# Two attention stages of a diffusion block: stages one step apart, SBUF divided by phase, TensorE in the emitted order

## The chip, the core and the metric

The kernel is one program on one core of a Trainium2 chip. The core has a matrix engine (PE, TensorE; PEld are its weight loads), a vector engine (DVE), a scalar engine (ACT), a general engine (POOL, GpSimd) and a queue engine (SP) from which most DMAs are issued. They run side by side, each through its own list of instructions in order, and wait for one another by semaphores. The metric is the device time of one execution in microseconds; lower is better.

## The reference

Two layers over 512 latent tokens and 256 context tokens of width 1024, all in float32. Layer 0 mixes tokens by differential attention (8 heads, each with two query and key maps of 64 and values of 128), layer 1 by a neighbourhood attention (16 heads, here in 8 groups of two). Each is followed by an MLP with hidden width 4096.

```python
def diff_attend(q, k, v, lam):                                  # layer 0
    s = einsum('bqhmd,bkhmd->bhmqk', q, k) * ATTN_SCALE          # two maps m
    p = softmax(s)
    return einsum('bhqk,bkhe->bqhe', p[:, :, 0] - lam * p[:, :, 1], v)
# layer 1, each query row: a window of keys with a bias and a mask, and all context keys
prob = softmax(concat([where(col_in, s_loc + bias, -inf), s_ctx]))
o = p_loc @ v_band + p_ctx @ v_c
# both layers
q, k = rms_norm(q, q_gain), rms_norm(k, k_gain)                  # per head, over 64
x = x + mod[2] * (o @ w_o)
x = x + mod[5] * (square(relu(modulate(rms_norm(x), mod[3], mod[4]) @ w1)) @ w2)
# mod = silu(c) @ w_mod + b_mod: six sections of 1024 columns for each layer
```

## The kernel before

Tokens lie in six tiles of 128 (two of context, four latent). A float32 product is done in three passes of a high and a low part, so every weight tile has a copy W[:, 0] (ACT, L99) and a remainder W[:, 1] (POOL, L100); its raw form arrives in a tile R, of which there are two. The loops are unrolled.

- **Start** (0 to 66 us): the first norm, the first modulation chunks and head 0's projections (`first_head`).
- **Layer 0 attention** (to 444 us): for each of 8 heads `qkv0` projects six token tiles (L346, 24 products of 384 columns each), norms q and k (`qk_normed`, L350), rotates them on POOL (L412 to L416), transposes (`turn`, L424) and splits them (`q_split`, `k_split`). `attend0` works on six query tiles: scores into the only PSUM tile S (L458), maxima (L463), exponentials (L464), the difference of the two maps (L470), transposes (L478), their split (L480, L481), the product with the values (L485), and the norm of the output (L487 to L494), which goes to DRAM as oT (L501).
- **Output projection, residual and norm** (`project`, L651), partly beside head 7's attention; then **MLP 0** (561 to 1111 us, L719 up and L753 down) with 24 modulation chunks beside it (L200 to L213), each one's weights loaded by SP.
- **Layer 1 attention** (1180 to 1495 us): `qkv1` and `attend1` for 8 groups, four units each (L575 to L618), with the bias by DMA (L514) and its mask added on POOL (L517). Then its projection, and **MLP 1** to the end.

What sets the order: the streams are Python generators, and `run` steps them by a string of letters (`ORD_HEAD` for a head, `ORD_GROUP` for a group), so that the projections of head h+1 are emitted among the attention of head h. This order gives only priorities. A planner (`schedule_with_timeline_sim=True`) simulates the engines and puts each engine's instructions, PE's too, in the order in which it finds them ready. A tile tag has a fixed number of buffers: five W of 1024 columns for the whole program, four N, seven Y, two each of E and X. One head's weights are four W. A new tile waits for the release of an old one.

Of the kernel before, what the change touches and what calls it, by code (L numbers as in the profile page):

```python
# [10 lines left out]
F32 = mybir.dt.float32  # L11
# [7 lines left out]
P = 128  # L19
D = 1024  # L20
# [14 lines left out]
# the order of the interleaved streams, by letters (see run)  # L35
ORD_FIRST = "aa"
# [13 lines left out]
class Block:  # L50
    def __init__(self, tc, ctx, a):
# [6 lines left out]
        self.wpool = pool("wpool", 5)  # L58
# [5 lines left out]
    BUFS = {"H": 8, "Q": 8, "E": 2, "X": 2, "N": 4, "Y": 7, "O": 4, "T": 2, "SQ": 12, "SA": 12, "SO": 8, "V": 1, "C4": 1}  # L64

    def sbt(self, tag, shape, dt=F32):
        self.n += 1
        return self.sb.tile(shape, dt, tag=tag, name=f"{tag}{self.n}", bufs=self.BUFS[tag])

# [21 lines left out]
    def wload(self, src, n, tile=None, eng=None):  # L91
        """a weight slice [128, n] as its float32r parts: [:, 0] high, [:, 1] low."""
# [4 lines left out]
        if w is None:  # L97
            w = self.wpool.tile([P, 2, 1024], F32R, tag="W", name=self._name("W"))
# [4 lines left out]
    def mod_load(self, l, n, early=False):  # L103
        """256 columns of the modulation matrix, as eight k-tiles."""
        src = self.a["wmod"][l, n]
        if early:
            w = self.wpool.tile([P, 2048], F32, tag="W", name=self._name("W"))
# [9 lines left out]
    def setup(self):  # L117
# [13 lines left out]
        # silu(c), silu(c_ctx), padded to 32 columns  # L131
# [8 lines left out]
        # modulation scalars: [layer][norm] -> A (gain*(1+scale)), B (shift)  # L140
# [28 lines left out]
        # lambda  # L169
# [221 lines left out]
    def qkv0(self, w, hT, out, accs=None, tag='Q'):  # L391
# [37 lines left out]
        for i, t in ((0, None), (1, None), (2, 0), (3, None), (4, 2), (5, None)):  # L429
            tile_(i)  # L430
            yield
            if t is not None:
                turn(t)
                yield
# [520 lines left out]
```

## Time and profile before

| | |
|---|---|
| runs | 1925.61, 1935.61, 1938.24 us; median 1935.61 |
| span of the profiled execution | 1928.0 us, 7.6 below the median; no other time is given for that execution |
| PE busy | 1809.4 us (94%) over 10256 matmuls |
| DVE, ACT, POOL busy | 1205.3, 812.5, 770.6 us (63%, 42%, 40%) |
| mean granted PE clock | 0.977 |
| HBM | 95 GB/s over the span |

A group row of the profile has line, engine, operation, output and inputs, shape and count; then the busy time, the mean in ns of one, and the engine's idle time before them with who ended it. A row of a windows view has the stretch, its length, the busy time and instruction count of PE, PEld, DVE, ACT and POOL, the granted PE clock, DMA share and GB/s. A row of a timeline has start and length in us. Matmuls overlap in the pipeline, so the time that one costs is the distance between starts, which is shorter than its listed duration. The heads' periods are read from the seven stores of oT (L501), the groups' from those of L621, of which those used here are at 223.8, 275.6, 327.5, 379.8 and 429.9 us, and at 1253.2, 1289.8, 1334.0, 1374.9, 1416.1 and 1458.0 us.

### The profile page before, as it was taken

The numbers are of one execution on the slowest core, as the hardware profiler recorded it, in microseconds if no ns is written. First come the engines' busy times: TensorE is split into PE (matmuls) and PEld (weight loads), VectorE is DVE, ScalarE is ACT, GpSimd is POOL, SyncE is SP. The second block draws the span as 40 slices with busy tenths as digits, with TensorE's granted clock in tenths as the row PEclk, the third lists the DMA queues.
The fourth block names the chain that finished last, engine by engine and source line by source line (L and its number), as shares of the span: only waits on it lengthen the run. The fifth ranks groups of instructions, "written<-read, shape, count | busy, mean of one in ns | idle before, by whom it ended". The sixth has DMA issues, their size and how long they took to land.

```text
span 1928.0 us, 27111 instructions
## 1 busy us (share of the span) xinstructions
PE 1809.4 (94%) x10256; PEld 1574.1 (82%) x10256; DVE 1205.3 (63%) x2349; ACT 812.5 (42%) x1819; POOL 770.6 (40%) x620
## 2 busy tenths in 40 slices
PE   6899999997899999999999988998998989999998
PEld 5788888885688888888888968998897778888886
DVE  4688888887664343343334685988889664444447
ACT  4466666666342221221221244666656342232231
POOL 3655555544222221221222443444543334344443
PEclk9999999998999999999999998999998999999999
DMA  7222222225222332332432241223323223323331
GB/s 296 92 67 71 86 85 74 73 69 195 84 89 90 118 120 91 128 124 95 131 113 74 57 125 41 50 62 74 77 72 99 93 77 100 97 87 94 103 94 71
DMA packets 58723, 185.02 MB, mean 96 GB/s; under 512 B 7328, under 2 KB 13792, under 8 KB 54496
## 3 DMA queue, kind: packets, MB, share of 16 engines
q1 hardware_dynamic: 52848, 173.44, 29.1%
q10 hardware_dynamic: 5744, 9.85, 1.4%
q8 instruction: 80, 1.31, 0.3%
q14 instruction: 51, 0.42, 0.1%
HBM read 174.45 MB, written 8.81 MB: 95 GB/s over the span
## 4 chain that ended last, share of the span: by engine, by line
PE 67%; DVE 15%; DMA 6%; ACT 4%; POOL 4%; issue 4%; SPq 1%; ACTq 0%; POOLq 0%; DVEq 0%
PE PD L719 23%; PE PA L753 11%; PE PB L753 10%; PE PA L346 9%; PE PA L651 4%; PE PA L200 2%; DMA X<-in_rpb_dram 2%; PE PS L458 2%; PE PB L485 1%; POOL W L100 1%; PE PQ L335 1%; DVE SA L581 1%; DMA N<-oT 1%; DMA R<-in_wmod_dram 1%; DVE N L604 1%
## 5 line engine op out<-in xcount | busy, mean ns | idle before, releaser
L100 POOL TENSOR_TENSOR W<-R,W 128x1024 fp32r<-128x1024 f32 (+1 forms) x200 | 451.0, 2262 | 700.8 <-ACT W L99 700.7
L99 ACT ACTIVATE W<-R 128x1024 fp32r<-128x1024 f32 (+1 forms) x204 | 200.9, 994 | 457.8 <-PE PB L753 364.2
L719 PE MATMUL PD<-Q,W 128*128 128x384 f32 (+1 forms) x1584 | 291.4, 332 | 1.1 <-DVE Q L270 0.5
L719 PEld LDWEIGHTS PD<-Q,W 128*128 128x128 f32 x1584 | 269.5, 188 | 16.6 <-issue 7.0
L346 PE MATMUL PA<-W,H 128*128 128x384 f32 x1008 | 201.8, 347 | 5.1 <-DVE T L209 4.4
L728 DVE TENSOR_TENSOR N<-N 128x768 f32<-128x768 f32 (+1 forms) x64 | 61.9, 969 | 220.3 <-ACT N L727 110.7
L346 PE MATMUL PA<-W,Q 128*128 128x384 f32 (+1 forms) x1008 | 186.7, 332 | 10.9 <-DVE H L535 5.6
L719 PE MATMUL PD<-H,W 128*128 128x512 f32 (+1 forms) x816 | 187.6, 386 | 3.4 <-DVE H L271 2.5
L346 PEld LDWEIGHTS PA<-W,H 128*128 128x128 f32 x1008 | 176.3, 191 | 13.0 <-DVE T L209 4.9
L719 PEld LDWEIGHTS PD<-H,W 128*128 128x128 f32 x816 | 148.9, 191 | 36.3 <-DVE H L271 2.7
L346 PEld LDWEIGHTS PA<-W,Q 128*128 128x128 f32 x1008 | 162.7, 198 | 13.3 <-DVE H L535 7.0
L753 PE MATMUL PA<-W,H 128*128 128x512 f32 x648 | 168.1, 399 | 2.7 <-DVE T L759 2.5
L233 POOL TENSOR_TENSOR SQ<-SQ,half 128x4 f32<-128x4 f32 (+1 forms) x96 | 93.9, 979 | 161.0 <-DVE SQ L231 133.9
L753 PEld LDWEIGHTS PA<-W,H 128*128 128x128 f32 x648 | 119.2, 188 | 32.9 <-issue 6.2
L753 PE MATMUL PB<-W,H 128*128 128x512 f32 x504 | 132.3, 394 | 0.0
L753 PE MATMUL PA<-W,Q 128*128 128x512 f32 x432 | 108.7, 391 | 2.2 <-ACT Q L730 1.7
L753 PEld LDWEIGHTS PB<-W,H 128*128 128x128 f32 x504 | 94.5, 188 | 19.4
L764 DVE TENSOR_TENSOR H<-PA,H 128x512 f32<-128x512 f32 x78 | 53.7, 688 | 78.6 <-PE PA L753 78.6
L753 PEld LDWEIGHTS PA<-W,Q 128*128 128x128 f32 x432 | 80.9, 188 | 21.1 <-ACT Q L730 2.4
L464 ACT ACTIVATE E<-PS,SA 128x768 f32<-128x768 f32 (+1 forms) x96 | 72.7, 758 | 34.4 <-DVE SA L463 33.8
L463 DVE TENSOR_REDUCE SA<-PS 128x1 f32<-128x768 f32 (+1 forms) x96 | 74.4, 775 | 20.2 <-ACT E L464 13.6
L753 PE MATMUL PB<-W,Q 128*128 128x512 f32 x336 | 85.3, 389 | 0.0
(213 smaller groups left out, 3177.1 us busy)
## 6 DMA issues: line engine op xcount, KB each, us to landing
R<-in_w_dram SPq DMA_DIRECT2D x128, 512.0 KB
W<-in_wmod_dram SPq DMA_DIRECT2D x32, 1024.0 KB
R<-in_wmod_dram SPq DMA_DIRECT2D x32, 512.0 KB
R<-in_wqa_dram SPq DMA_DIRECT2D x32, 384.0 KB
R<-in_wqb_dram SPq DMA_DIRECT2D x32, 384.0 KB
X<-in_rpb_dram SPq DMA_DIRECT2D x48, 128.0 KB
R<-in_woa_dram SPq DMA_DIRECT2D x8, 512.0 KB
R<-in_wob_dram SPq DMA_DIRECT2D x8, 512.0 KB
```

Of the source, the lines that this page charges most:

```text
L99: nc.scalar.activation(w[:, 0, :n], raw, AF.Copy)
L100: (eng or nc.gpsimd).tensor_sub(w[:, 1, :n], raw, w[:, 0, :n].bitcast(F32))
L200: nc.tensor.matmul(ps[32 * q:32 * q + 32, 0:256], self.silu[:, kt, :], raws[kt], start=kt < 4, stop=kt >= 4)
L233: nc.gpsimd.tensor_tensor(r, ss, self.half[:, :n], op=ALU.pow)
L346: nc.tensor.matmul(acc[:, :n], hT[kt][:, x, P * i:P * i + P], w[kt // 2][:, y, o:o + n], start=(kt == 0 and p == 0), stop=(kt == KT - 1 an ...
L463: nc.vector.tensor_reduce(mx, s, op=ALU.max, axis=AX, negate=True)
L464: nc.scalar.activation(e[:, m, :nk], s, AF.Exp, bias=mx[:, 0:1], accum_out=sm[:, m:m + 1])
L651: nc.tensor.matmul(ps, oHL[h][:, x, c:c + P], w[h // 2][:, y, 512 * (h % 2):512 * (h % 2) + 512], start=(h == hs[0] and p == 0), stop=(h = ...
L719: nc.tensor.matmul(ps[:, at:at + b1 - b0], w[kt // 4][:, x, o:o + P], hT[kt][:, y, b0:b1], start=(kt == 0 and p == 0), stop=(kt == KT - 1 ...
L728: nc.vector.tensor_mul(r, r, r)
L753: nc.tensor.matmul(ps, hd[:, x, P * i - c0:P * i - c0 + P], w[f][:, y, 512 * n:512 * n + 512], start=(f == 0 and p == 0), stop=(f == len(h ...
L764: nc.vector.tensor_add(av, ps, av)
```

## The change

It keeps the arithmetic and regroups it. (1) `sbuf_phase` gives W, N and a new tag OT to pools that are opened and closed with four phases: five W of 1024 columns and four N at the start and around both MLPs, eight W of 768 and two OT in layer 0's attention, six W of 768 and four N in layer 1's. Y has six buffers in place of seven. (2) `attend0` and `attend1` are cut into the stages scores (0), turned (1) and weigh (2), emitted in the order of ATT0 and ATT1; `qkv0` and `qkv1` step in halves of a token tile; the last turn of a head is emitted inside the next head's loop (`p`), and the first two tiles of a group inside the group before (`r`). A head's weights are asked for one loop earlier. (3) Both loops run under `manual_schedule` for PE: its instructions keep the emitted order; the other engines' are still placed by the planner. The start, the first group's projections, both output projections and both MLPs are outside it. (4) Some DVE operations change: the addition of EPS after the q and k norm's sum becomes a 65th column of that sum, four operations become `scalar_tensor_tensor`, and the copy at L385 moves to POOL. (5) Four of the 24 modulation chunks beside MLP 0 move to the end of layer 1's attention. The output projection steps in four and three heads.

```diff
-ORD_HEAD = "qlalmqmaqqaqbqqbqaAQ"
-ORD_OUT0 = "lmlmaqaqaqAQ"
-ORD_GROUP = "qaqqaqaqaqAQ"
-ORD_OUT1 = "aqaqaqaAQ"
+ORD_HEAD = "aa qq aa q p q l a q a q m l a qq a q aaa q m aaa qq a q b a q aa"
+ORD_OUT0 = "q l aaaa p a m l a m a q a q aaa q aaa qq a q a qq aa Q"
+ORD_FIRST1 = "qqqqqqqqqqqq rr q a"
+ORD_GROUP = "qq a q a qq a a q a q a aa qqq a a r q a r b"
+ORD_GROUP7 = "qq a q a qq a a q a q a aa l qqq a a m q a b"
+ORD_OUT1 = "q a l a m a l aa m a q aa q a q a qq a l m Q"
+MODS_LATE = 4
+ATT0 = ((0, 1), (1, 0), (2, 0), (1, 1), (2, 1), (0, 2), (0, 3), (1, 2), (2, 2), (0, 4), (1, 3), (2, 3),
+        (0, 5), (1, 4), (2, 4), (1, 5), (2, 5))
+ATT1 = ((0, 1), (1, 0), (2, 0), (0, 2), (1, 1), (2, 1), (0, 3), (1, 2), (2, 2), (1, 3), (2, 3))
...
+    def sbuf_phase(self, name, wcols, **tags):
+        with ExitStack() as st:
+            self.wcols, self.bufs = wcols, tags
+            self.room = {tag: st.enter_context(self.tc.tile_pool(name=name + tag, bufs=n, reuse_waits="tile"))
+                         for tag, n in tags.items()}
+            yield
...
     def qk_normed(self, acc, ns):
-        sq = self.sbt('Y', [P, n])
-        nc.scalar.activation(sq, raw, AF.Square, scale=0.125)
+        nc.scalar.activation(self.sq[:, :ns, 0:64], xn, AF.Square, scale=0.125)
-        nc.vector.tensor_reduce(ss, sq.rearrange("p (a b) -> p a b", b=64), op=ALU.add, axis=AX)
-        r = self.rstd(ss, ns, 'SQ')
-        nc.vector.tensor_mul(xn, xn, r[:, :, None].to_broadcast([P, ns, 64]))
+        nc.vector.tensor_reduce(ss, self.sq[:, :ns], op=ALU.add, axis=AX)
+        r = self.power(ss, ns, 'SQ')
+        nc.vector.scalar_tensor_tensor(xn, xn, 1.0, r[:, :, None].to_broadcast([P, ns, 64]),
+                                       op0=ALU.mult, op1=ALU.mult)
...
-            nc.vector.tensor_copy(kl[b, m, cols], kl[a, m, cols].bitcast(F32))
+            nc.gpsimd.tensor_copy(kl[b, m, cols], kl[a, m, cols].bitcast(F32))
...
+        for i in range(NT):
+            acc = self.pst('A')
+            for half in range(2):
+                self.qkv_matmul(acc, half, w, hT, i, 0, 384)
+                if half == 1:
+                    tile_(i, acc)
+                yield
+                if (i, half) in ((3, 0), (4, 1)):
+                    turn(0 if i == 3 else 2)
+                    yield
         turn(4)
         yield
...
-            nc.vector.tensor_scalar_mul(on, o, ro[:, 0:1])
+            nc.vector.scalar_tensor_tensor(on, o, ro[:, 0:1], self.one[:, 0:1].to_broadcast([P, P]),
+                                           op0=ALU.mult, op1=ALU.mult)
...
+        scores(0)
+        yield
+        for stage, i in ATT0:
+            (scores, turned, weigh)[stage](i)
             yield
         turn(*late.pop(0))
...
-                nc.vector.tensor_sub(u[:, 1, :], r, u[:, 0, :].bitcast(F32))
+                nc.vector.scalar_tensor_tensor(u[:, 1, :], r, 1.0, u[:, 0, :].bitcast(F32),
+                                               op0=ALU.mult, op1=ALU.subtract)
...
-            for h in range(1, HEADS0):
-                nxt = []
-                qkv = b.qkv0(w if h == 1 else b.load_qkv(a["wqa"], h), hT, nxt)
-                att2 = b.attend0(h, nxt, last if h + 1 == HEADS0 else None)
-                run(mods, ORD_HEAD, q=qkv, a=att, b=att2)
-                att = att2
+            run(mods, "a", a=att)
+            ahead = iter(())
+            with tc.manual_schedule(engines={mybir.EngineType.PE}):
+                for h in range(1, HEADS0):
+                    nxt = []
+                    qkv = b.qkv0(w, hT, nxt)
+                    if h + 1 < HEADS0:
+                        w = b.load_qkv(a["wqa"], h + 1)
+                    att2 = b.attend0(h, nxt, last if h + 1 == HEADS0 else None)
+                    run(mods, ORD_HEAD, q=qkv, a=att, b=att2, p=ahead)
+                    att, ahead = att2, qkv
...
+                if len(mods.todo) > MODS_LATE:
+                    mods.load(True)
+                    mods.chunk()
...
+            with tc.manual_schedule(engines={mybir.EngineType.PE}):
+                for g in range(1, GROUPS1):
+                    att2 = b.attend1(g, nxt, last if g + 1 == GROUPS1 else None)
+                    qkv, nqkv, nxt = nqkv, None, []
+                    if g + 1 < GROUPS1:
+                        nqkv = b.qkv1(b.load_qkv(a["wqb"], g + 1), hT1, nxt)
+                    run(mods, ORD_GROUP if nqkv else ORD_GROUP7, q=qkv, r=nqkv, a=att, b=att2)
+                    att = att2
```

The fourth operation that becomes `scalar_tensor_tensor` is the copy of 64 columns at L589.

More of the change, by code (lines that the diff above doesn't have):

```diff
@@ L619, in attend1 @@
+        scores(0)
+        yield
+        for stage, u in ATT1:
+            (scores, turned, weigh)[stage](u)
+            if (stage, u) != ATT1[-1]:
                 yield
@@ L671, in project @@
             ps = self.pst('A')
[L672 removed]
+            part(ps, w0, i, range(4), final=False)
+            yield
+            part(ps, w0, i, range(4, KT - 1), first=False)
             gated(ps, x, i, 0, x)
```

245 lines of the change are left out of this document (137 added, 108 removed).

## The prediction

> **What bounds the kernel now.** I read the page first, then the windows view over whole periods, then PE's timeline for the price of one matmul, and last DVE's groups and the chain of waits.
>
> ```profile
> PE 1809.4 (94%) x10256; PEld 1574.1 (82%) x10256; DVE 1205.3 (63%) x2349; ACT 812.5 (42%) x1819; POOL 770.6 (40%) x620
> ...
> PE 67%; DVE 15%; DMA 6%; ACT 4%; POOL 4%; issue 4%; SPq 1%; ACTq 0%; POOLq 0%; DVEq 0%
> ```
>
> PE is busy for 94%, which leaves 119 us, yet a third of the chain that ended last is not PE's. The two don't fit, because a listed matmul is longer than what it costs. So I price PE's work by distances between starts. The windows view gives the sums over five chunks of MLP 0 (698.35 to 883.2), four heads (223.8 to 429.9) and five groups (1253.2 to 1458.0), and one group:
>
> ```profile
> sum 184.85, PE 184.85 PEld 158.09 DVE 70.51 ACT 39.13 POOL 47.71; mean PE 36.97 PEld 31.62 DVE 14.10 ACT 7.83 POOL 9.54
> ...
> sum 206.10, PE 193.52 PEld 175.49 DVE 170.85 ACT 136.91 POOL 109.24; mean PE 48.38 PEld 43.87 DVE 42.71 ACT 34.23 POOL 27.31
> ...
> sum 204.80, PE 189.54 PEld 184.46 DVE 177.57 ACT 129.67 POOL 94.65; mean PE 37.91 PEld 36.89 DVE 35.51 ACT 25.93 POOL 18.93
> ...
> 1289.80:1334.00 44.20, 39.20 (x264) 38.45 (x263) 36.22 (x88) 26.63 (x68) 19.46 (x20) 0.92 0.24 60
> ```
>
> PE's timeline, in MLP 0, a head and a group:
>
> ```profile
> 738.89 0.50 PE L213 MATMUL PA<-sel,T 128*128 128x2 f32 x4
> 739.25 8.05 PE L719 MATMUL PD<-Q,W 128*128 128x384 f32 x45
> 747.24 1.07 PE L200 MATMUL PA<-W,silu 128*32 128x256 f32 x16
> 748.24 1.65 PE L753 MATMUL PA<-W,H 128*128 128x512 f32 x6
> 749.73 2.96 PE L753 MATMUL PB<-W,H 128*128 128x512 f32 x12
> 752.52 0.88 PE L719 MATMUL PD<-Q,W 128*128 128x384 f32 x4
> ...
> 257.99 0.49 PE L478 MATMUL PB<-ident,E 128*128 128x128 f32 x3
> 258.23 1.30 PE L346 MATMUL PA<-W,H 128*128 128x384 f32 x6
> ...
> 263.24 1.59 PE L485 MATMUL PB<-Q,X 128*128 128x256 f32 x12
> 264.67 0.27 PE L446 MATMUL PB<-ident,O 128*128 128x128 f32 x1
> 264.70 5.17 PE L346 MATMUL PA<-W,H 128*128 128x384 f32 x28
> 269.71 1.57 PE L458 MATMUL PS<-Q,Q 128*128 128x512 f32 x8
> 271.11 1.76 PE L346 MATMUL PA<-W,H 128*128 128x384 f32 x9
> ...
> 1361.61 0.45 PE L612 MATMUL PB<-N,H 128*128 128x256 f32 x3
> 1361.89 0.39 PE L612 MATMUL PB<-N,V 128*128 128x128 f32 x2
> 1362.12 0.62 PE L602 MATMUL PB<-ident,E 128*128 128x128 f32 x4
> 1362.49 3.23 PE L346 MATMUL PA<-W,Q 128*128 128x384 f32 x17
> ```
>
> From start to next start: 384 columns cost 5.01/28 = 0.179 us in a head and 7.99/45 = 0.178 in the MLP; 512 cost 2.79/12 = 0.233; 256 cost 1.43/12 = 0.119 (0.093 in L612's run); a transpose 0.24/3 = 0.08 to 0.37/4 = 0.093; a tile's scores of 768 keys 1.40; a modulation chunk 0.50 + 0.36 = 0.86.
>
> Dense price of an MLP 0 chunk: 96 x 0.178 + 72 x 0.233 + 2 x 0.86 = 35.6. It takes 36.97, 4% more, with PE never idle: that is as dense as PE gets here.
> Dense price of a head: 144 x 0.179 = 25.8 for the projections, 4 x 1.40 + 8 x 0.119 = 6.6 for scores, 56 x 0.119 = 6.7 for the values, 40 transposes x 0.08 = 3.2, six L446 at 0.03 = 0.2, two chunks 1.7: 44.2. It takes 206.10/4 = 51.5.
> Dense price of a group: 96 x 0.179 + 48 x 0.119 = 22.9, scores 32 x 0.119 = 3.8, values 24 x 0.093 + 16 x 0.115 = 4.1, 42 transposes x 0.093 = 3.9: 34.7. It takes 204.80/5 = 41.0.
>
> So a head holds 7.3 us and a group 6.3 us beyond the dense price. DVE is busy for 42.7 of 51.5 (83%) and 35.5 of 41.0 (87%): PE waits for chains that run through a nearly full DVE. The row with 0.92 shows that the clock falls in the gaps too (44.2 x 0.08 = 3.5 us of full clock in that group).
>
> By the Trainium skill ("Perfetto Trace Analysis", Identifying the Most-Contended Engine) the share of weight loads tells how near PE is to its peak. By that share heads (43.87 of 51.5, 85%) and MLP 0 (31.62 of 36.97, 86%) would be equally full, and this change would have no room. I don't follow it, since a head's loads serve narrower matmuls; it is a rival below.
>
> **The change, part by part.** DVE's groups in the four heads, ACT's behind the scores, and three prices from the whole run:
>
> ```profile
> L463 DVE TENSOR_REDUCE SA<-PS 128x1 f32<-128x768 f32 x32 | 30.6, 955 | 7.0 <-ACT E L464 6.0 <-PE PS L458 0.4
> L470 DVE SCALAR_TENSOR_TENSOR E<-E,SA 128x768 f32<-128x768 f32 x16 | 16.8, 1051 | 0.4
> L361 DVE TENSOR_TENSOR Y<-Y,SQ 128x256 f32<-128x256 f32 x24 | 14.3, 596 | 2.6 <-POOL SQ L233 2.2
> L385 DVE CAST Q<-Q 64x256 fp32r<-64x256 f32 x24 | 11.5, 478 | 0.8
> L494 DVE TENSOR_SCALAR O<-O,SO 128x128 f32<-128x128 f32 x24 | 11.2, 465 | 4.8 <-POOL SO L233 4.5
> L231 DVE TENSOR_SCALAR SQ<-SQ 128x4 f32<-128x4 f32 x25 | 7.1, 286 | 0.4
> L470 DVE SCALAR_TENSOR_TENSOR E<-E,SA 128x256 f32<-128x256 f32 x8 | 4.2, 522 | 0.1
> ...
> L464 ACT ACTIVATE E<-PS,SA 128x768 f32<-128x768 f32 (+1 forms) x48 | 36.4, 757 | 17.0 <-DVE SA L463 16.6
> ...
> L489 DVE SCALAR_TENSOR_TENSOR O<-PB,SA,O 128x128 f32<-128x128 f32 x48 | 16.6, 347 | 5.2 <-ACT O L488 4.6
> ...
> L556 POOL CAST V<-H 64x256 fp32r<-64x256 f32 x16 | 6.9, 431 | 27.4 <-PE PB L612 21.5 <-DVE H L535 5.4
> ...
> L731 DVE TENSOR_TENSOR H<-N,H 128x768 fp32r<-128x768 f32 x13 | 25.5, 1963 | 4.8 <-ACT H L730 4.8
> ```
>
> *DVE operations.* Each head loses six L231 (7.1/4 = 1.8) and six L385 (11.5/4 = 2.9), and saves 6 x (596 - 522) and 6 x (465 - 347) ns = 1.1: 5.8 of 42.7 us. POOL gains 6 x 0.43 = 2.6 on 27.3. A group loses, at the head's means, 6 x (0.286 + 0.478) = 4.6 of 35.5. L731 falls from 1963 to about L470's 1051 ns, but in MLP 0 DVE works 14.1 of 37 us and PE doesn't wait: 0. L589 and the 65th column: 0, inside these.
>
> By the Trainium skill ("SBUF — State Buffer", Who interferes with whom) any DVE instruction with two SBUF inputs is held by a POOL instruction that reads SBUF, so L361's new form would save nothing. L470 has two such inputs and its mean of 1051 ns hardly shows it; if the page held, 0.4 us of DVE time per head would stay, and PE's sum would be the same.
>
> *Stages and PE's fixed order.* A wait of PE now holds every later PE instruction, so each stage must be covered by what is emitted before it. Scores to next scores, with one tile S: two maxima and the second exponential, 2 x 0.955 + 0.76 = 2.7, say 3.0 us with the signals between; the closest pair (tiles 2 and 3) is covered by half a tile, 2.15, and a chunk, 0.86: even, perhaps 0.5 late. Scores to turned adds L470, about 4.5 us; cover 6.5 or more: 0. Turned to weigh: an ACT and a DVE pass over 384 columns, each shorter than L464, so under 1.5 us; cover 2.1 or more: 0. The last turn to scores of tile 2: cover 4.8 us, need some 3, or 5 behind a weight split on POOL: 0 taken, at most one split of 1.78 (below) late. The 65-column tile has one buffer, free after one L358: 0. In layer 1 the chain from scores to turned is of the same kind and covered by 6 us or more: 0. I give a head 4% over 44.2, as MLP 0 has, and 1.0 for late stages: 47.0. A group: 4% over 34.7 and 0.9: 37.0. The bounds for a head are 44.2 + 1 and 51.5, for a group 35.5 and 41.0; a loss is a rival.
>
> *Weights and bias.* Eight W let a head's weights land a whole loop ahead; six let half of a group's. The chain shows what waits for it now:
>
> ```profile
> 275.68 1.78 POOL W L100
> 277.48 4.92 DMA R<-in_wmod_dram
> ...
> 1223.79 5.45 DMA X<-in_rpb_dram
> ...
> 457.90 6.79 DMA N<-oT
> ```
>
> These are inside the 4.5 us of a head and 4.0 of a group. Before, the bias load stands on SP behind weight loads that wait for a W; with two W ahead SP is free for it. The reopened pools add waits for the tiles that lay there: bounds 0 and one landing of about 5 us at each of three boundaries; I take 0, as the raw tiles R stay and land meanwhile.
>
> *Ends.* Loop 7 of each layer and the projection behind it, from the last store counted above:
>
> ```profile
> 429.90:568.00 138.10, 120.57 (x603) 95.51 (x602) 92.51 (x181) 67.42 (x160) 47.16 (x37) 0.91 0.37 124
> 1458.00:1562.00 104.00, 87.57 (x445) 72.28 (x443) 77.82 (x145) 51.55 (x107) 37.08 (x25) 0.91 0.32 104
> ```
>
> Idle and clock leave 17.5 + 12.4 and 16.4 + 9.4 us. Head 6 and group 6 finish earlier in the fixed order, so oT's read-back (6.79 above) comes earlier; against that nearly all of the last head's attention is left with no projections beside it. I take -10 and -8; bounds -20 to +8 and -16 to +8.
>
> *Late chunks.* Four leave a dense MLP 0: -4 x 0.86 = -3.4. At layer 1's end the 16.4 idle us cover them; without these, +3.4.
>
> **Sum.** Six full loops of each layer lie between these ends: 6 x (51.5 - 47.0) = 27, 6 x (41.0 - 37.0) = 24, ends 18, chunks 3.4: 72. The span of 1928.0 becomes 1856. The median of the runs is 7.6 above that span: 1863.
>
> **Rivals.**
> *Denser still.* If DVE's share is the limit, periods fall by what DVE loses: 6 x 5.8 + 6 x 4.6 = 62 for 51, 1852. With both at their lower bounds, 6 x 6.3 + 6 x 5.5 = 71, and ends -36: 1825. For it: 83% and 87%. Against: PE's order can't use what is ready early. Chance 0.21, about 1840.
> *A DMA at the head of PE's order.* Raw tiles R remain two, and four weight loads stand on SP before each chunk's two. The first chunk comes some 16 us into the head (six halves at 2.15 and the stages between) and waits for splits (4 x 1.78 on POOL) and a landing of up to 4.92. At 2.5 us per head, seven times: +17, 1880. Against: so far PE lost little there. Chance 0.12.
> *No room.* If the excess is how PE runs narrow matmuls, only the late chunks are gained: 1932. For it: the weight loads' share. Against: the MLP has 4%, a head 17%. Chance 0.11.
> *Slower.* DVE's list is in order and still about 80% full, and PE now stands behind each late stage. One late stage costs its whole delay: at 0.35 us for each of 17 stages of a head and 12 of a group the gain of the loops is gone, and each further 0.1 us costs 6 x (1.7 + 1.2) = 17. At 0.5 us the time is 1936 + 26 = 1962. For it: L361 and L494, held by POOL for over 0.1 us on average. Against: the covers above. Chance 0.08.
>
> **How the numbers follow.** The forecast has 0.48 and its own range is 1840 to 1890. The range of 1820 to 1915 takes in the denser case and the waiting chunks and leaves out the last two rivals: about 2 in 10. About 1% is what a measurement of this kernel tells from no change: faster 0.48 + 0.21 + 0.12 = 0.81, the same 0.11, slower 0.08.
>
> **What would show it.** Right: stores of oT every 47 and 37 us; DVE near 37 us per head; PE idle behind L200 and the scores small; no bias or weight load on the chain inside the loops; a clock of 1.00 there. Wrong: PE waiting for L464 before scores or for L481 before the values in every head; L200 waiting for its load; gaps at the pool boundaries; ends longer than 138 and 104 us.

## The result, and the profile after

The changed kernel takes 2018.56 us (median; 2014.8 to 2021.36) beside 1935.65 us of the kernel before on the same chip: a ratio of 1.044, 95% interval [1.0418, 1.0462]. It is 4.4% slower. The forecast was 1863 us, and the bottom of its chances, the slower rival with 0.08, came true.

The page of the kernel after: its span, the engines' busy time, and the chain that ended last.

```profile
span 2017.6 us, 27149 instructions
...
PE 1814.1 (90%) x10256; PEld 1588.0 (79%) x10256; DVE 1156.3 (57%) x2159; ACT 810.3 (40%) x1819; POOL 808.7 (40%) x716
...
PE 67%; DVE 11%; POOL 7%; issue 5%; ACT 5%; DMA 3%; SPq 0%; ACTq 0%; POOLq 0%; DVEq 0%
```

The span grew by 89.6 us, while PE's busy time grew by 4.7. DVE's busy time fell by 49.0 (1205.3 to 1156.3), but not in the head loops, as the second row of each view below shows (249.43 before, 250.69 after). POOL's share of the chain rose from 4 to 7%.

Where the time came from is seen in the windows view, cut at the same events in both kernels but for the first: the first projection of head 1 in the kernel before, the first store of oT0, the seventh, the first matmul of MLP 0, its last, the first and the seventh store of oT1, the first matmul of MLP 1. Columns: stretch, its length, busy time (and instructions) of PE, PEld, DVE, ACT, POOL, the granted clock, DMA share, GB/s. Before:

```profile
66.70:168.90 102.20, 91.84 (x576) 81.77 (x577) 85.41 (x206) 62.93 (x185) 57.83 (x69) 0.97 0.20 61
168.90:473.80 304.90, 277.77 (x1805) 246.42 (x1804) 249.43 (x592) 205.08 (x580) 160.83 (x190) 0.97 0.30 95
473.80:561.00 87.20, 80.53 (x376) 64.04 (x376) 52.02 (x101) 32.23 (x73) 20.93 (x16) 0.96 0.22 73
561.00:1149.70 588.70, 584.93 (x3251) 506.73 (x3249) 271.66 (x378) 144.07 (x203) 176.53 (x86) 1.00 0.34 108
1149.70:1253.20 103.50, 89.32 (x583) 84.84 (x584) 80.32 (x203) 55.82 (x148) 43.93 (x46) 0.93 0.21 52
1253.20:1491.70 238.50, 216.03 (x1434) 206.77 (x1433) 208.68 (x483) 151.21 (x378) 107.08 (x109) 0.94 0.29 76
1491.70:1555.90 64.20, 58.86 (x285) 48.14 (x284) 40.61 (x74) 26.89 (x54) 19.84 (x13) 0.95 0.24 75
```

After (the first stretch begins at nearly the same time, 66.8, while head 1's projections start at 102.2 only):

```profile
66.80:162.80 96.00, 56.48 (x337) 50.05 (x338) 65.48 (x125) 48.93 (x135) 58.84 (x67) 0.77 0.23 69
162.80:524.60 361.80, 301.64 (x1957) 276.72 (x1956) 250.69 (x551) 207.00 (x601) 176.50 (x236) 0.92 0.22 69
524.60:636.60 112.00, 97.48 (x462) 75.68 (x462) 64.70 (x123) 44.07 (x101) 33.51 (x24) 0.90 0.32 104
636.60:1215.70 579.10, 575.33 (x3179) 506.52 (x3178) 268.18 (x374) 141.62 (x197) 175.11 (x85) 1.00 0.32 102
1215.70:1304.00 88.30, 73.51 (x471) 69.17 (x472) 60.24 (x143) 49.57 (x125) 43.85 (x50) 0.91 0.26 61
1304.00:1554.80 250.80, 226.11 (x1549) 219.06 (x1547) 178.52 (x431) 149.75 (x388) 113.72 (x148) 0.97 0.28 66
1554.80:1645.10 90.30, 72.79 (x352) 53.88 (x353) 52.04 (x92) 36.58 (x73) 30.95 (x20) 0.87 0.38 123
```

The six head loops take 56.9 us more, layer 0 around them 18.7 more (-6.1 at its front, counted from the span's start, +24.8 at its end), the six groups 12.3 more, layer 1 around them 10.9 more (-15.2, +26.1); MLP 0 gives 9.6 back. These are 89.2 of the 89.6 us. Front and end of a layer go together: a store that comes earlier in the loop shortens the one and lengthens the other. A head's period is 61.2 us on average over the first four loops (first to fifth store, 162.8 to 407.7); a group's is 42.7 over the first five (1304.0 to 1517.4), or 42.2 in the median.

What PE waited for in the head loops (162 to 456 us) and in the groups (1290 to 1520) of the kernel after; columns: what waited, on whom, us in total, times, longest:

```profile
PE PB L480 <- DVE O L536: 36.8, 9, 5.2
PE PA L235 <- ACT T L225: 8.8, 8, 1.3
PE PA L227 <- ACT T L225: 2.5, 2, 1.6
...
PE PA L589 <- DVE Y L383: 10.9, 5, 2.4
PE PB L662 <- DVE T L683: 8.2, 6, 2.5
PE PS L632 <- POOL H L407: 6.5, 5, 1.9
```

L480 transposes a head's normed output. Its last two stand at the end of the loop, and one loop end of the kernel after shows the rest. PE's timeline there (start, length, instruction, in brackets the idle time before it and what ended it):

```profile
274.02 1.69 PE L527 MATMUL PB<-Q,X 128*128 128x256 f32 x12 [0.42 <-DVE X L519]
278.55 0.45 PE L480 MATMUL PB<-ident,O 128*128 128x128 f32 x1 [2.83 <-DVE O L536]
284.06 0.45 PE L480 MATMUL PB<-ident,O 128*128 128x128 f32 x1 [5.07 <-DVE O L536]
```

DVE's timeline at the same place:

```profile
278.06 0.34 DVE L536 SCALAR_TENSOR_TENSOR O<-O,SO,one 128x128 f32<-128x128 f32 x1
278.61 0.15 DVE L252 TENSOR_SCALAR SO<-SO 128x1 f32<-128x1 f32 x1 [0.21 <-ACT O L534]
278.90 2.01 DVE L383 SCALAR_TENSOR_TENSOR Y<-Y,SQ 128x256 f32<-128x256 f32 x1
282.04 1.88 DVE L536 SCALAR_TENSOR_TENSOR O<-O,SO,one 128x128 f32<-128x128 f32 x1 [1.12 <-POOL SO L258]
```

POOL's:

```profile
278.83 1.80 POOL L117 TENSOR_TENSOR W<-R,W 128x768 fp32r<-128x768 f32 x1
280.60 0.90 POOL L437 TENSOR_TENSOR Y<-Y,Y 128x256 f32<-128x256 f32 x1
281.46 0.54 POOL L258 TENSOR_TENSOR SO<-SO,half 128x1 f32<-128x1 f32 x1
281.97 1.80 POOL L117 TENSOR_TENSOR W<-R,W 128x768 fp32r<-128x768 f32 x1
```

And the windows view around it, where the figure behind POOL's busy time is the granted clock:

```profile
276.00:278.00 2.00, 0.00 (x0) 0.00 (x0) 1.28 (x4) 1.73 (x4) 1.78 (x4) 1.00 0.62 178
278.00:280.00 2.00, 0.45 (x1) 0.18 (x1) 1.66 (x4) 1.50 (x4) 2.00 (x2) 0.59 0.05 18
...
287.00:288.00 1.00, 1.00 (x5) 1.00 (x4) 0.33 (x3) 0.57 (x2) 0.00 (x0) 0.50 0.57 221
288.00:289.00 1.00, 1.00 (x6) 1.00 (x5) 0.72 (x2) 0.00 (x0) 0.00 (x0) 0.69 0.21 78
```

The sum of squares is ready at 278.76 (L252). Its power on POOL (L258) waits for a weight split (L117) and a rope step until 281.46, and DVE's product (L536) starts as POOL begins the next split and takes 1.88 us, a little longer than that split. PE stands for 2.83 and 5.07 us, 7.9 us a loop, and what it does from 284.06 to 288.6 it does at half clock: by estimate 2.3 us more. 61.2 - 7.9 - 2.3 is 51.0.

### The profile page after: what moved, and what is told of

The parts are those of the page before. It is cut to its first block, busy times and chain, and to the rows that moved or that the text cites. A ratio compares the mean times of both kernels' runs of the same rounds, so it can differ in the third digit from the quotient of the medians.

```text
span 2017.6 us, 27149 instructions
## 1 busy us (share of the span) xinstructions
PE 1814.1 (90%) x10256; PEld 1588.0 (79%) x10256; DVE 1156.3 (57%) x2159; ACT 810.3 (40%) x1819; POOL 808.7 (40%) x716
## 4 chain that ended last, share of the span: by engine, by line
PE 67%; DVE 11%; POOL 7%; issue 5%; ACT 5%; DMA 3%; SPq 0%; ACTq 0%; POOLq 0%; DVEq 0%
PE PD L794 21%; PE PA L370 11%; PE PA L829 11%; PE PB L829 9%; PE PA L723 3%; POOL W L117 2%; PE PA L222 2%; POOL SQ L258 1%; PE PS L492 1%; POOL X L566 1%; PE PB L677 1%; PE PB L527 1%; PE PQ L360 1%; ACT E L498 1%; DVE SA L497 1%
## 5 line engine op out<-in xcount | busy, mean ns | idle before, releaser
L117 POOL TENSOR_TENSOR W<-R,W 128x1024 fp32r<-128x1024 f32 (+1 forms) x200 | 449.5, 2255 | 643.5 <-ACT W L116 629.6
L803 DVE TENSOR_TENSOR N<-N 128x768 f32<-128x768 f32 (+1 forms) x64 | 64.4, 1008 | 223.5 <-ACT N L799 117.1
L370 PEld LDWEIGHTS PA<-W,H 128*128 128x128 f32 x1008 | 185.1, 199 | 1.0
L258 POOL TENSOR_TENSOR SQ<-SQ,half 128x4 f32<-128x4 f32 (+1 forms) x96 | 97.1, 1012 | 212.2 <-DVE SQ L381 210.5
L370 PE MATMUL PA<-W,Q 128*128 128x384 f32 (+1 forms) x1008 | 177.4, 331 | 1.1 <-POOL W L117 1.1
L829 PEld LDWEIGHTS PA<-W,H 128*128 128x128 f32 x648 | 119.3, 188 | 30.0 <-issue 4.5
L498 ACT ACTIVATE E<-PS,SA 128x768 f32<-128x768 f32 (+1 forms) x96 | 72.9, 760 | 72.4 <-DVE SA L497 72.2
L497 DVE TENSOR_REDUCE SA<-PS 128x1 f32<-128x768 f32 (+1 forms) x96 | 74.5, 776 | 32.8 <-ACT E L498 18.5
L492 PE MATMUL PS<-Q,Q 128*128 128x256 f32 (+1 forms) x320 | 71.5, 360 | 22.3 <-ACT E L498 12.0
```

What stands on the lines that cost most here:

```text
L117: (eng or nc.gpsimd).tensor_sub(w[:, 1, :n], raw, w[:, 0, :n].bitcast(F32))
L258: nc.gpsimd.tensor_tensor(r, ss, self.half[:, :n], op=ALU.pow)
L370: nc.tensor.matmul(acc[:, :n], hT[kt][:, x, P * i:P * i + P], w[kt // 2][:, y, o:o + n], start=(kt == 0 and p == 0), stop=(kt == KT - 1 an ...
L492: nc.tensor.matmul(s[:, c0:c1], q[:, m, P * i:P * i + P], k[:, m, c0:c1], start=p == 0, stop=p == 1)
L497: nc.vector.tensor_reduce(mx, s, op=ALU.max, axis=AX, negate=True)
L498: nc.scalar.activation(e[:, m, :nk], s, AF.Exp, bias=mx[:, 0:1], accum_out=sm[:, m:m + 1])
```

## The experiments

**The order taken away.** The first set gives PE back to the planner in layer 0, in layer 1, in both, or keeps the order and moves the last two output transposes and the store into the next loop (letter z, behind the first projections).

```
-            with tc.manual_schedule(engines={mybir.EngineType.PE}):
+            if True:
```

```
-            if len(late) > 1:
+            if len(late) > 1 and i < NT - 1:
...
-        turn(*late.pop(0))
+        while late:
+            turn(*late.pop(0))
...
-ORD_HEAD = "aa qq aa q p q l ... q b a q aa"
+ORD_HEAD = "aa qq aa q p q z l ... q b a q a"
```

> The changed kernel without the fixed PE order in layer 0's loop; the planner orders PE there as it did before, layer 1 keeps the fixed order. Theory (the fixed order is what costs in layer 0; stages, pools and DVE operations don't): the stretch from the first norm's end to MLP 0, 570 us, returns to 495 to 510, the time to 1945 to 1960. Rival (the reopened pools and weights loaded a loop ahead are what costs, for they hold POOL and SP): the stretch stays over 550, the time over 1995.

> The changed kernel without the fixed PE order in layer 1's loop; layer 0 keeps it. Theory: the stretch of layer 1 from its first turn to MLP 1, 407 us, returns to the 384 of before or less, since PE no longer stands at the scores (for the k copy on POOL) and at the last turn: time 1990 to 2000. Rival (layer 1's extra time is at its end, from the late modulation chunks and the reopened pools): stretch over 400, time over 2008.

> The changed kernel without any fixed PE order; stages, pools, DVE operations and late chunks as changed. Theory: all of the loss goes, and what the other parts give remains: 1915 to 1945, within 1% of before. Rival (other parts of the change cost by themselves): over 1960.

> The changed kernel, with the last two transposes of a head's output (L480, tiles 4 and 5) and its store emitted in the next head's loop, behind three and a half projection halves, in place of at the end of its own. Theory (in the fixed order PE stands at these transposes, 7.9 us per loop, and the clock halves for 10 us behind them): a head's period falls from 61.2 to 48 to 50 us, the granted clock in the loops rises from 0.92 to 0.98 or more, the time falls from 2018 to 1935 to 1960. Rival (the two transposes only show that DVE and POOL are late by then, so the wait moves to the next stage in the order): period 57 or more, time 1990 or more.

Layer 0 free: 1961.05 us, ratio to the kernel before 1.0144 [1.0118, 1.0169], heads 51.4 us. Layer 1 free: 2005.7, 1.0373 [1.0346, 1.0399], groups 39.6 in the median. Both: 1952.31, 1.0097 [1.0078, 1.0117]. So the fixed order costs 66 of the 83 us (58 and 13 singly), and some 17 us aren't its doing. None of the three lands in the range of a theory: with layer 0 free the time is 1 us above it, with layer 1 free and with both free it lies between theory and rival. Late transposes: 1996.14, 1.0323 [1.03, 1.0345], heads 58.1: the rival was right. The wait of L480 is gone from the head loops, and half of it stands at the next stage; the largest wait of PE in the head loops of that run:

```profile
PE PC L445 <- POOL Y L437: 19.4, 5, 3.9
```

L445 turns q and k of the last two tiles, and the rope step that it needs (L437) stands in POOL's list behind the four weight splits.

**POOL's list.** The splits fall at the loop's end because eight W hold two heads' weights: the loads are emitted ahead of a loop, land early, and can be split only when the loop before has read its weights for the last time. The next set issues each of them behind a modulation chunk (letter w), without and with late transposes, moves k's copy back, and tries another order in layer 1.

```
-                        w = b.load_qkv(a["wqa"], h + 1)
+                        ws = b.load_steps(a["wqa"], h + 1, w)
...
-ORD_HEAD = "... q m l a qq a q aaa q m aaa ..."
+ORD_HEAD = "... q m ww l a qq a q aaa q m ww aaa ..."
...
-            nc.gpsimd.tensor_copy(kl[b, m, cols], kl[a, m, cols].bitcast(F32))
+            nc.vector.tensor_copy(kl[b, m, cols], kl[a, m, cols].bitcast(F32))
...
-ORD_GROUP = "qq a q a qq a a q a q a aa qqq a a r q a r b"
+ORD_GROUP = "qq a q a qq a q a a q a qq aaa q a r a r a q"
...
```

> The changed kernel, but the four weight loads of the head after next are issued one by one behind the two modulation chunks of a loop, not ahead of the loop: so their splits (L116, L117, four of 1.8 us on POOL, now at 270 to 284 in the loop that ends at 284.9) leave POOL's list at the loop's end. Theory, that POOL's list sets half of the wait at the last output transposes: the wait of L480 falls from 7.9 to about 4.5 us a loop, the period from 61.2 to 56 or 57 us, 1990 us. It doesn't vanish, since weigh, ScalarE's square, VectorE's add, POOL's power and VectorE's product stand in a row with nothing of TensorE's behind them. Rival, that the row alone makes the wait, not what POOL does beside it: L480 7 us or more, period 60 or more, 2010 us or more.

> Both together: the last two output transposes of a head stand in the next loop, and the weight loads are spread as in the run beside it. Theory: with late transposes alone the wait went to L445, 3.9 us a loop behind the four weight splits on POOL; without them there, no wait of over 1 us at the loop's end is left, the clock stays whole, period 50 or less, layer 0 shorter by 45 us or more than in the changed kernel: 1955 to 1975 us. Rival, that the last turn's chain (copy, square, sum, power, product and three rope steps) is longer than the work between by itself: L445 still waits for 2.5 us or more, period 56 or more, 1985 us or more.

> The changed kernel with one part undone: the copy of k's low parts (L407) is on VectorE again, all else as changed. Theory, that POOL's list is what TensorE meets at the ends of the loops: the wait of L632 for L407 in layer 1 (6.5 us in five groups, 1.3 us each) goes, the groups come from 42.2 to 41 us and the heads from 61.2 to 60 or less; 2000 to 2010 us. Rival, that POOL's copies lay in time that POOL had free and VectorE is the scarcer engine: the six copies cost VectorE some 2 us a head, its waits at L480 and L589 grow by as much, and the time is 2018 to 2030 us.

> The changed kernel with other letters in the orders of layer 1 alone: the first scores of a group stand after the second projection step of the next loop in place of the loop's end, and the last turn of q and k stands ahead of the last two stages. Theory, that a fixed order costs what its stages have too little cover for: the waits of L589, L662 and L632 (5.1 us a group) fall to about 2, the groups come from 42.2 to 39 us, 2018 to 1996 us in all. Rival, that the chain by POOL and VectorE behind each group is as long as the loop's work allows and any fixed order meets it somewhere: the wait shows under another name, groups of 41.5 us or more, 2012 us or more.

Spread alone: 1987.65, 1.0274 [1.0256, 1.0293], heads 57.0 over five loops (149.7 to 434.9), as the theory had it. Both: 1956.86, 1.0124 [1.0105, 1.0142], 61.7 us below the changed kernel, more than the two alone (22.4 and 30.9); heads 51.1 over four loops, where the theory had 50 or less. The largest wait of PE in the head loops (162 to 456 us) with the spread alone, where L485 is L480 and L541 is L536:

```profile
PE PB L485 <- DVE O L541: 15.7, 5, 3.2
```

The three largest with both edits, where L532 is L527:

```profile
PE PA L235 <- ACT T L225: 7.5, 8, 1.6
PE PA L227 <- ACT T L225: 3.8, 4, 1.5
PE PB L532 <- ACT OT L486: 3.7, 5, 0.7
```

Without the splits the row of work behind the last values still costs 3.1 us a loop, with them 7.9. So both causes are shown: a row with nothing to cover it, and POOL's list within the row. The clock adds to both: it is 0.93 over the five loops with the spread alone, and 1.00 over the four with both edits. One loop of the kernel after, in the windows view:

```profile
224.10:284.90 60.80, 49.87 (x327) 46.02 (x327) 42.26 (x90) 34.64 (x100) 30.77 (x41) 0.92 0.21 68
```

And one with both edits:

```profile
209.00:259.90 50.90, 47.71 (x327) 44.23 (x327) 37.47 (x90) 34.49 (x101) 31.84 (x41) 1.00 0.26 81
```

The same instructions, the clock whole, PE busy for 47.7 of 50.9 us. K's copy on DVE: 2007.24, 1.0374 [1.0355, 1.0392], 11 us less; heads 58.3, but groups 43.3, not 41 as expected: L632's wait is gone there, and L589's grew (10.9 to 13.5 us). The other order in layer 1: 2028.4, 1.0496 [1.0473, 1.052], groups 44.6: the rival was right, L589's wait only grew (10.9 to 16.7 us).

**Forms, late chunks, the front.** The four DVE operations as before; MODS_LATE = 0; and, on top of both edits, the first loop outside of the fixed order.

```
-        nc.vector.scalar_tensor_tensor(xn, xn, 1.0, r[:, :, None].to_broadcast([P, ns, 64]),
-                                       op0=ALU.mult, op1=ALU.mult)
+        nc.vector.tensor_mul(xn, xn, r[:, :, None].to_broadcast([P, ns, 64]))
...
-MODS_LATE = 4
+MODS_LATE = 0
...
-            with tc.manual_schedule(engines={mybir.EngineType.PE}):
-                for h in range(1, HEADS0):
+            for h in range(1, HEADS0):
+                with nullcontext() if h == 1 else tc.manual_schedule(engines={mybir.EngineType.PE}):
```

> The changed kernel with the four VectorE products and differences written as before again (L383, L536, L646, L806: tensor times tensor, scalar product, copy, difference, in place of scalar_tensor_tensor). Theory, that the new form gains nothing and gives the operation that waits behind POOL a longer time: L383 takes 960 ns in the heads' loops as changed and 610 ns as before, L536 710 and 450; both stand in the row that ends at the waits of L445, L480 and L589, so these shrink by 0.3 to 0.6 us each and the time by 5 to 10 us, to 2008 to 2014. Rival of the prediction, that the new form escapes POOL's hold: with the old forms VectorE is busier by 5 us a head, and the time is 2020 us or more.

> The changed kernel with the modulation chunks of layer 1 back in the first MLP: none is left to the ends of layer 1 (MODS_LATE 0 in place of 4; the letters l and m in the orders of layer 1 then do nothing). Theory, that the chunks cost more at the end of layer 1 than they save in the MLP: the MLP takes 588 us in place of 579, the stretch from its end to the second MLP 414 us or less in place of 429.5, and the time falls by 5 us or more, to 2013 or less. Rival, the prediction's: they are covered there, only the MLP's 9 us come back, 2023 to 2028 us.

> Late transposes and spread loads, and the first of the seven head loops outside of the fixed order. In the changed kernel TensorE is busy for 7 of the 37 us ahead of the first projections of the second head, since the order puts the first head's scores and values, whose splits and rope are not done, ahead of them. Theory, that this idle time is lost to the whole: the projections start at 67 in place of 96 us, and the first MLP starts 10 us or more earlier than the 574.8 us of the run without it: 1935 to 1948 us. Rival, that the first loop is as long by the other engines' work for the first head anyway: 572 us or more, 1952 us or more.

Old forms: 2019.13, 1.0432 [1.0402, 1.0461], no difference. DVE's groups in the head loops of the changed kernel (count, busy us, mean ns, idle before and its releaser):

```profile
L383 DVE SCALAR_TENSOR_TENSOR Y<-Y,SQ 128x256 f32<-128x256 f32 x29 | 25.1, 866 | 7.1 <-POOL SQ L258 6.5
...
L536 DVE SCALAR_TENSOR_TENSOR O<-O,SO,one 128x128 f32<-128x128 f32 x29 | 19.3, 666 | 9.5 <-POOL SO L258 9.1
```

The same with the old forms:

```profile
L383 DVE TENSOR_TENSOR Y<-Y,SQ 128x256 f32<-128x256 f32 x29 | 23.8, 822 | 6.8 <-POOL SQ L258 5.9
...
L535 DVE TENSOR_SCALAR O<-O,SO 128x128 f32<-128x128 f32 x29 | 17.6, 607 | 9.4 <-POOL SO L258 9.0
```

The two forms are alike within 10% in the same place; before, the same operations took 609 and 445 ns. The place made them longer: in the kernel after, 8 of the 29 L383 take 2.0 us and 4 of the 29 L536 1.88, each beside a weight split on POOL, and the others under 0.9. With the loads spread, none of them is that long:

```profile
L383 DVE SCALAR_TENSOR_TENSOR Y<-Y,SQ 128x256 f32<-128x256 f32 x32 | 13.5, 423 | 9.2 <-POOL SQ L258 8.9
```

Both the theory (a cost) and its rival (a gain) were wrong.

No late chunks: 2016.29, 1.0412 [1.0384, 1.044], an interval that overlaps the changed kernel's. In the profile MLP 0 goes from 579.1 to 587.8 us and the stretch from there to MLP 1 from 429.4 to 417.0: the chunks weren't covered there, and cost at least what they saved. The time lies between theory and rival. The front: 1963.2, 1.0138 [1.0112, 1.0163]; head 1's projections start at 64.4 in place of 95.9, and MLP 0 at 577.5 in place of 574.8. The rival was right: the idle front isn't lost to the whole. That the first head's stages are done in it, and later ones not held up, fits but wasn't shown.

**A version that would pay.** Late transposes, spread loads, free first loop and layer 1, no late chunks and the old forms in one; then, each on top of the one before: the chunk in two stages (a yield behind L225's copy, letter n for a half); no chunks at layer 0's end (and the MLP's gates loaded at its end); k's copy on DVE.

```
         nc.scalar.activation(sb, ps[:, 0:256], AF.Copy)
+        yield
...
-ORD_HEAD = "... q m ww l a qq a q aaa q m ww aaa ..."
+ORD_HEAD = "... q n ww l a n qq a q aaa q n ww a n aa ..."
...
-ORD_OUT0 = "z q l aaaa p a m l a m a q ..."
+ORD_OUT0 = "z q aaaa p a a a q ..."
```

> The edits that the runs so far speak for, in one: late transposes, spread loads, first loop and layer 1 outside of the fixed order, no chunk left to layer 1's ends, the old VectorE forms. If the costs found singly add up (62 us by the first two, 10 by the front, 12 by layer 1, 5 by the chunks, 5 by the forms): 1915 to 1930 us, a little below the kernel before. If the ends, which none of these edits touches (22 us longer at layer 0 and 20 at layer 1 than before, from the seventh store to the MLP), grow by what the loops lose, as the planner run's ends did: 1940 to 1955 us.

> The mixed run, with each modulation chunk of the head loops in two stages: the eight first products and ScalarE's copy, then, one stage of the attention later, the second products (L227, L235). Theory, that a stage of a fixed order with a copy between its own products waits for all of it: the 13 us that L235 and L227 wait for ScalarE in the seven loops fall under 2, the period from 50.9 to 49 us, 1944 to 1930 us. Rival, that what stood there is met again at the next wait of the loop, since POOL, VectorE and ScalarE set its length: period 50.5 or more, 1940 us or more.

> The run beside it, with the two modulation chunks at the end of layer 0 left to the first MLP (and the MLP's gates loaded at its end, since these chunks make them). Theory, that the end of layer 0 is held by DMA: the projection's first products start at 478 us or earlier in place of 485, the stretch from the seventh store to the MLP falls from 111 to 100 us or less, the MLP takes 4 us more by its two chunks: 5 to 8 us faster than the run beside it. Rival, that the stretch is held by the attention's late stages and the weights' place in the reopened pools: it falls by the chunks' own products, 4 us, and the MLP gives them back: within 3 us of the run beside it.

> The run without chunks at layer 0's end, and the copy of k's low parts (L407) back on VectorE. Theory, that the copy on POOL cost 11 us in the changed kernel only because POOL's list was full where TensorE waited: with the loads spread it costs nothing, and the time is within 4 us of the run beside it. Rival, that it costs wherever q and k are turned, as POOL takes 0.4 to 0.7 us for a copy and holds VectorE meanwhile: another 6 to 10 us faster.

In one: 1944.34, 1.0053 [1.0034, 1.0071], the second of the two expectations. Chunk in two stages: 1949.7, 1.0077 [1.0059, 1.0095], heads 51.3; the rival was right. The two largest waits of PE in the head loops (110 to 467 us) and the chunk's other one, without the cut, where L496 is L492 and L502 is L498:

```profile
PE PS L496 <- ACT E L502: 7.9, 10, 3.9
PE PA L235 <- ACT T L225: 7.5, 8, 1.5
...
PE PA L227 <- ACT T L225: 3.9, 4, 1.6
```

And the largest with it (L497 and L503 there):

```profile
PE PS L497 <- ACT E L503: 14.7, 10, 3.9
```

The chunk's 11.4 us of waits are gone, and the scores, which have one PSUM tile, wait for the exponential 6.8 us longer. No chunks at the end: 1967.47, 1.0173 [1.0148, 1.0198]; the end shrinks by only 5 us and MLP 0 grows by 18, not 4; so neither theory nor rival held, and whether the two chunks or the gates' late load did that wasn't told apart. K's copy on DVE there: 1964.85, 1.0143 [1.0117, 1.0169], within 4 us as the theory had it: with POOL's list short, the copy costs nothing that can be measured.

**The end of layer 0.** The base is the mixed version with the first loop in the order and the forms as changed; then the last head's loop outside of the order, or in an order with its projections two by two:

```
+                with nullcontext() if h + 1 == HEADS0 else tc.manual_schedule(engines={mybir.EngineType.PE}):
...
+ORD_HEAD7 = "aa qq aa qq p qq z l a qq a qq m l a qq a qq aaa m aaa a b a a"
```

> The base of the two runs beside it: late transposes, spread loads, layer 1 outside of the fixed order, no chunk left to layer 1's ends; first loop in the fixed order and VectorE's forms as changed. By the runs so far the first loop (578 against 575 us at the MLP's start) and the forms (2019 against 2018) are worth nothing, so within 5 us of the mixed run's 1944 us; 1935 or less if the first loop in the fixed order is better, as one profile had it.

> The run beside it, with the loop of the last head outside of the fixed order. Theory, that the reopened pools hold the end of layer 0 until head 7's last projection is done: the order left free puts these projections ahead, as in the planner run (435 us, 45 ahead of the seventh store), the output's weights are split 10 to 20 us earlier, and the first MLP starts 5 to 12 us earlier than in the run beside it. Rival, that head 7's attention chain sets the end: its stages then come later by as much, and the MLP starts within 3 us or later.

> The first run, with the projections of head 7 two by two early in its loop, still in a fixed order: the last one comes some 12 us earlier. Theory of the pools: the splits of the output's weights and the first of its products come 8 us or more earlier, and the first MLP starts 5 us or more earlier. Rival, the attention's chain: the same products of head 7's scores and values stand at the end, with less between them, and the MLP starts within 3 us or later.

Base: 1939.16, 1.0019 [1.0007, 1.0032], 5.2 us below the mixed version. Last loop free: 1935.09, 1.0006 [0.9994, 1.0017]. Projections early: 1932.23, 0.9991 [0.998, 1.0001]. The first split of the output's weights on DVE comes at 454.4, 444.3 and 448.3 us, in the first two 2 us behind head 7's last projection, but MLP 0 starts at 574.6, 573.8 and 572.6: the rival was right both times, and the place in the reopened pools isn't what holds that end. From the sixth to the seventh store and from there to MLP 0, in the windows view of the base:

```profile
363.90:464.60 100.70, 87.74 (x595) 79.04 (x594) 74.52 (x172) 66.17 (x188) 55.98 (x74) 0.97 0.29 96
464.60:574.60 110.00, 96.76 (x460) 75.78 (x461) 63.68 (x123) 43.95 (x101) 32.71 (x24) 0.92 0.33 106
```

And with the projections early:

```profile
363.30:470.50 107.20, 94.48 (x628) 82.95 (x627) 76.94 (x177) 68.39 (x195) 58.44 (x76) 0.95 0.33 109
470.50:572.60 102.10, 90.65 (x435) 72.02 (x428) 64.06 (x118) 41.70 (x94) 31.35 (x21) 0.93 0.28 94
```

Work only moves over the seventh store: 210.7 and 209.3 us for both rows. No version is measurably faster than the kernel before. In the last one layer 0 is still a loss: MLP 0 starts 11.6 us later than before (572.6 for 561.0), though 10 earlier than with the changed stages in the planner's order (582.7). What makes up for it is layer 1, in the planner's order: from MLP 0's last product to MLP 1 it takes 397.8 us for 406.2 before. In the base, whose layer 1 has the same source, that stretch takes 406.1; why the two differ wasn't looked into.

## Why the prediction was wrong

**The step that failed** is "Stages and PE's fixed order", with its "1.0 for late stages". It listed the pairs from scores to weigh and gave each its cover. It left out the row that leaves PE behind the last values: square, sum, power, product, then L480. In the order the last tile's row has no cover at all; the row of the tile before it has some (PE works until 275.7), and its wait of 2.83 us is gone when the splits are spread. Together they cost 7.9 us a loop and the clock an estimated 2.3 more. The slower rival named the mechanism (a late stage costs its whole delay) but took it as even, 0.35 us in each of 17 stages; in fact one stage had 36.8 of the 52.0 us that PE waited between 162 and 456 us, and 0.08 was far too little for a list of covers that wasn't complete. Its price of 1962 starts from 1936, though only the loops' 51 us were taken as lost: with the ends and chunks as forecast its own sum is 1940.

The measured span is 162 us above the forecast one (2017.6 and 1856). In the terms of the sum 77 of them lie in the loops and 91 in the ends, and MLP 0 gained 6 more than forecast. The fixed order alone makes 66 of the 83 us of loss; what makes the rest is open.

**The last turn.** The cover of "the last turn to scores of tile 2" was put at 4.8 us: "need some 3, or 5 behind a weight split on POOL: 0 taken", and at most one split late. With L480 out of the way this was the next wait, 3.9 us, behind four splits. The prediction counted POOL's busy share, not where in the loop its work falls; the eight W, costed as a gain, put the four splits at the loop's end.

**K's copy on POOL** was costed at 2.6 us a head of an engine with time to spare, so at 0. It cost 11 us in all, for the same reason (without it PE's wait at L480 is 27.1 us for 36.8), and nothing measurable once the list was short.

**The size of a dense head was nearly right.** 46.0 was forecast without lateness (44.2 and 4%); PE is busy for 47.7 us of a loop that has no long wait. The loop is 50.9 and not 47: waits of 3.2 us are left in it, and what one of them (the chunk's) gives up, another (the exponential's) takes, as the run with the cut chunk showed. So 51.5 would have become 50.9, hardly a gain.

**Groups**: forecast 37.0, got 42.7 on average; the three waits listed above are 5.1 us of it (25.6 us over five). Neither order tried was better than the planner's, which gave 40.0 on average with the same stages (39.6 in the median).

**The other rivals.** The chunk's load never held PE in the loops after (L222 is not among the waits), and the weight loads' share, 44.23 of 50.9 us (87%), stands in a loop that still has 3.2 us idle. That speaks against "no room", but no run made use of those 3.2 us, and the best version, at 1932, happens to be where that rival put the time: it isn't ruled out. Of the signs of being wrong in "What would show it" only the longer ends came; the wait that did come was not among them, as the list was made from the same pairs as the covers.

**Ends** is the term with the largest miss: forecast -18, measured +72.6. From the sixth store, where the prediction cut, to the MLP it took 131.1 us before (429.9 to 561.0) and 173.9 after (462.7 to 636.6) in layer 0, 97.9 and 127.7 in layer 1. Of the 42.8 us in layer 0, 18.0 lie in its last head loop (sixth to seventh store, 43.9 to 61.9), under the same fixed order. With both layers in the planner's order the two stretches are 14.4 and 15.2 longer than before, so some 43 of the 72.6 us go with the order. "Head 6 and group 6 finish earlier in the fixed order" is what failed there: the sixth store of layer 0 came 32.8 us later. That of layer 1 came 6.6 us earlier, counted from MLP 0's end, and its end grew all the same. In layer 1 the late chunks are part of the rest: forecast to be covered by 16.4 idle us, they took 12.4 and gave MLP 0 8.7. What lengthens the end of layer 0 stays open: not the order alone (free, it grew too), nor the reopened pools, nor mainly the chunks. The stage order of the kernel before wasn't tried at that end.

**DVE.** A head's load did not fall in the kernel after: 42.4 us a head over the four loops, for 42.7 before. With the loads spread it is 37.9, near the 36.9 worked out, and 37.5 in the loop shown with both edits. The difference of 4.5 is what the splits held: over those four loops L383 takes 959 ns on average and L536 706, for 423 and 493 with the loads spread, six of each a head. What that fall alone was worth isn't shown. L731, forecast to fall from 1963 to 1051 ns, kept its length (mean over the run 1685 before, 1635 after; priced at 0). The reading that scalar_tensor_tensor escapes POOL's hold was wrong: it rested on L470's mean, and L470's rows name no release by POOL, while those of L361 and L494 do. The page of the Trainium skill that the prediction set aside ("SBUF — State Buffer", Who interferes with whom) was right: two SBUF inputs are held, whatever the form. The trace agrees: 1.88 and 2.01 us beside splits of 1.80. So is the old form of the output's product, with one 128x128 input and a scalar: 1.81 us beside a split of 1.80 in the run with the old forms.

## What to carry to other kernels

Before an engine is put into a fixed order, write down every chain that leaves it and comes back, the short one at the end of a loop too, and count its cover in that order; one chain without cover can cost more than all that the order was to gain (here 10.2 us a loop, where the order and the rest were to gain 4.5). Cost a helper engine by its list at the moment when the chain passes through it, not by its busy share: four splits a loop on POOL, moved from the loop's end to its middle, gave back 30.9 us of the run. Where removing one wait lets another grow by most of it, as in the run with the cut chunk, more cover for that wait gains nothing.

## What the runs showed of the hardware

The clock fell to half at about 278.4 (0.59 over 278 to 280), 2.7 us after PE's last matmul had ended by the profile (275.7), and was whole again at about 288.6 (0.69 over 288 to 289), 4.5 us after work had resumed at 284.06. By the Trainium skill ("TensorE: Matmul & The Clock Gate", Part 1) full clock comes back after about 4 us of sustained work, which agrees, and is lost after an idle window of about 3.4 us; here the gap at the fall was shorter. The two waits of 7.9 us so cost an estimated 10.2.

The DVE products that started just behind a weight split on POOL lasted about as long as the split: 128x128 elements took 1.88 us beside a split of 1.80, and 0.34 us four microseconds earlier in the same loop, beside a POOL operation on 128x4 elements (L258).
